# Hybrid state-space and attention layer on one core: state-space products with 512-column high parts, gate sigmoids taken at the merge, two heads' outputs summed together

## The chip, the core and the metric

The program runs on one core of a Trainium2 chip. The core has a matrix engine (TensorE, in profile rows PE, its weight loads PEld), three engines for element-wise work (VectorE = DVE, ScalarE = ACT, GpSimd = POOL) and DMA queues (SP's carries the weights here, POOL's most of the rest). Each engine works through its own list of instructions in order; semaphores tie the lists together. The metric is the device time of one execution in microseconds (us).

## The reference

One decoder layer on 256 tokens of width 2048, all in float32. The part that matters here:

```python
h = rmsnorm(x, attn_norm_w)
z, xbc, dt_raw, q, k, v, g = split(h @ w_in)
xbc = silu(causal_dwconv(xbc, conv_w, conv_b))           # 4 taps along the tokens
xs, Bm, Cm = split(xbc)                                  # 4096 + 1024 + 1024 channels
y = (cb * decay) @ (xs * dt) + xs * d_skip               # per group of 8 heads; head width 64
yg = y * silu(z); yg = yg * rsqrt(mean(yg*yg) + eps) * norm_w
y_ssm = yg @ w_ssm_out
g_ssm, g_attn = split(sigmoid(g + b_gate))
x = x + (g_ssm * y_ssm + g_attn * y_attn) @ w_out
x = x + ffn(rmsnorm(x))                                  # up, 3-tap conv, silu gate, down
```

There are 8 groups of the state-space branch. Each has 4 tiles of z, 4 of xs, one of B and one of C, every tile 128 channels by 256 tokens. `cb * decay` is the 256x256 lower-triangular matrix of a head.

## The kernel before

**Products in three parts.** A float32 weight w is split into a rounded high part (`whi`, made by ACT, L198) and the rest (`wlo`, made by DVE, L199). The activations are split in the same way. A product is high·high + high·low + low·high, each in the fast float32 mode of TensorE. A "unit" (`cm_unit`, L243) is one 128-channel output tile: one weight tile of 128x2048 (1 MB) arrives in `wraw`, is split in two halves ("chunks") of 1024 columns, and each chunk is 8 weight blocks of 128x128. `cm_chunk` (L226) multiplies them in one of two forms:

- *narrow* (`wide=False`): per high block two matmuls of 256 columns, first against the activations' high part (L237), then against their low part (L238), both added into one 256-column result;
- *wide*: per high block one matmul of 512 columns (L234), which holds the high part's product in columns 0 to 255 of a PSUM bank and the low part's in columns 256 to 511. The two halves must be added afterwards by whoever reads the result.

In both forms the 8 low blocks then follow with one matmul of 256 columns each (L240). `wraw`, `whi` and `wlo` have three buffers each, counted in weight tiles for the first and in chunks for the other two; the results (`mm`) have four PSUM banks, and four more (`cc`) serve the state-space core.

**Stages.** Values, queries, keys and attention; the attention gates and the attention output (wide); then the state-space stage, about 455 to 1183 us of the span; then the output projection and the feed-forward network (both wide).

**The state-space stage** is a loop of nine steps (from L944). Step s < 8 computes the ten units of group s (`group_units`, L776), all narrow. The four z units (i < 4) are copied out by ACT (L781). The other six go through the 4-tap convolution: ACT writes the last tap plus bias (L785), and DVE adds three shifted taps (L788). While step s runs, the core of group s-1 is spread over its units, one entry of a list of 14 (`core_steps`, L792) per unit: SiLU of the group's ten tiles, with table loads on ACT (L798, L800); transposes; the decay matrices (`dec`, L842 on: Relu, Exp, multiply by `cb`, split into `mhl`); and `ydot` (L866), which multiplies them with xs for two heads at a time. `ydot(0)` to `ydot(3)` follow units 4, 6, 8 and 9. Per head it reads a PSUM bank with two interleaved halves: 64 partitions hold the head's high and low sums, the other 64 partitions a third part, and DVE adds x·d_skip and the three (L877, L879, L880), on 64 partitions each. Then comes the group's RMS norm. In steps 1, 2 and 8 there are also 4, 4 and 8 units for the state-space gates (`gate_ssm`, L932): ACT adds the bias and takes the sigmoid of the first 8 (L939), which go to DRAM in pairs through the buffer `g`; the last 8 stay in `pre[0]` without sigmoid (L936). From step 3 on there are four `out_unit`s per step (w_ssm_out, narrow, unchanged). At the end `merge` (L968) loads the saved gates back, takes the late ones' sigmoid, multiplies and adds.

**What sets the order.** The program is written unit by unit; a scheduler of the framework then orders each engine's list, keeping the order in which buffers are handed out. The buffer `g` (three of 256 KB) is shared by the attention gates, the state-space gates and the merge.

Of the kernel before, what the change touches and what calls it, by code (L numbers as in the profile page):

```python
# [8 lines left out]
F32 = mybir.dt.float32  # L9
F32R = mybir.dt.float32r  # L10
AF = mybir.ActivationFunctionType
# [4 lines left out]
DM, T, DI, G, NS, H, HD, DFF = 2048, 256, 4096, 8, 128, 16, 128, 5632  # L16
# [160 lines left out]
def _body(tc, nc, d, out):  # L177
# [103 lines left out]
    def sm(name, i=0, n=1, rows=slice(0, 128)):  # L281
        o, _ = _SMALL[name]
        return small[rows, o + i:o + i + n]
# [492 lines left out]
    def group_units(g):  # L776
        pr = pre[g % 2]
        for i in range(10):
            ps = cm_unit(d["wssd"][g, i], hnt, wide=False)
            if i < 4:  # L780
                S.activation(pr[:, i], ps, AF.Copy)  # L781
            else:
                ti = 4 * g + i - 4 if i < 8 else (32 + g if i == 8 else 40 + g)
                acc = pr[:, i]
                S.activation(acc, ps, AF.Identity, scale=sm("conv_w", 4 * ti + 3), bias=sm("conv_b", ti))  # L785
                for k in (2, 1, 0):
                    sh = 3 - k
                    V.scalar_tensor_tensor(acc[:, sh:], ps[:, :T - sh], sm("conv_w", 4 * ti + k), acc[:, sh:],  # L788
                                           op0=MUL, op1=ADD)
            yield i  # L790

    def core_steps(g):  # L792
# [73 lines left out]
        def ydot(p):  # L866
            def f():
                m = st.pop(("m", p))
                for h in range(2):
                    pt = c_tile().rearrange("p (t a) -> p t a", a=2)  # L870
                    ps = pt.rearrange("p t a -> p a t")
                    x0, x1 = [st["x"][:, s, p, 2 * h:2 * h + 2].rearrange("p a c -> p (a c)") for s in range(2)]
                    mt = m[:, :, h].rearrange("p a t -> p t a")
                    PE.matmul(pt, x0, mt[:, 0:256], start=True, stop=False)  # L874
                    PE.matmul(pt[:, 128:], x1, mt[:, 256:384], start=False, stop=True)  # L875
                    rs, ls = slice(h * 64, (h + 1) * 64), slice(64 - h * 64, 128 - h * 64)
                    V.scalar_tensor_tensor(yz[rs, p], pr[rs, 4 + p], sm("ssm_d", 4 * g + p, 1, rs), ps[rs, 0],  # L877
                                           op0=MUL, op1=ADD)
                    V.tensor_tensor(yz[rs, p], ps[rs, 1], yz[rs, p], op=ADD)  # L879
                    V.tensor_tensor(yz[rs, p], ps[ls, 0], yz[rs, p], op=ADD)  # L880
                if p % 2:
                    V.tensor_tensor(yz[:, p - 1:p + 1], yz[:, p - 1:p + 1], pr[:, p - 1:p + 1], op=MUL)
            return f
# [46 lines left out]
        return f  # L930

    def gate_ssm(o):  # L932
        pg = cm_unit(d["wgs"][o], hnt, wide=False)
        if o >= 8:

            S.activation(pre[0][:, o - 8], pg, AF.Identity, bias=sm("b_gate", o))  # L936
            return
        g = gate_half(o)
        S.activation(g, pg, AF.Sigmoid, bias=sm("b_gate", o))  # L939
        if o % 2:  # L940
            nc.gpsimd.dma_start(gs[o // 2], gpair.pop(o // 2))

    dt_steps(dt_unit())
# [24 lines left out]
    def merge(u, ps):  # L968
        os_ = slice(2 * u, 2 * u + 2)
        if u < 4:  # L970
            g = gate_pool.tile([128, 2, T], F32, name="g", bufs=3)
            nc.gpsimd.dma_start(g, gs[u])
            late = pre[0][:, 2 * u:2 * u + 2]
            with tc.issue_after(last_rsq[0].ins):
                S.activation(late, late, AF.Sigmoid)
        else:
            g = pre[0][:, 2 * u - 8:2 * u - 6]
# [135 lines left out]
```

## Time and profile before

| | us |
|---|---|
| median of 3 runs (lowest, highest) | 1967.05 (1965.49, 1968.47) |
| the profiled execution, whole | 1965.37 |
| its span on the core | 1963.6 |
| PE / DVE / ACT busy in the span | 1955.8 / 1567.6 / 1207.6 |
| state-space stage, 455.6 to 1182.7: PE / DVE / ACT busy | 725.4 / 629.3 / 503.8 of 727.1 |

The granted TensorE clock was 1.00 in every stretch. The matmul rows overlap each other, since matmuls are pipelined and the ends are modelled: what a matmul costs is read from the distance between starts, not from its own duration. The same holds in part for DVE and ACT, whose neighbouring rows overlap by some tens of ns.

### The profile page before, as it was taken

Reading aid. Unit: us, or ns where it says so; the run is one execution under the profiler, and the core shown is the slowest. Engines: PE = TensorE matmul, PEld = TensorE weight load, DVE = VectorE, ACT = ScalarE, POOL = GpSimd, SP = SyncE. Lnnn points to the kernel's source line nnn. Section 1 sums busy time; section 2 is a strip of 40 time slices with the busy share of each in tenths; the row PEclk is TensorE's granted clock in tenths of the full one; section 3 lists DMA queues with packets and bytes.
Section 4 is the critical chain, followed back from the end, with each engine's and each line's share of the span. In section 5 each row is a group of like instructions: output and inputs, shape, how many; then the busy total and the mean of one; then the engine's idle time right before and its main releaser. Section 6 shows DMA issues by size and latency. Waiting matters only on the chain.

```text
span 1963.6 us, 35306 instructions
## 1 busy us (share of the span) xinstructions
PE 1955.8 (100%) x14323; PEld 1861.7 (95%) x14323; DVE 1567.6 (80%) x2399; ACT 1207.6 (62%) x1758; POOL 78.6 (4%) x100
## 2 busy tenths in 40 slices
PE   9999999999999999999999999999999999999999
PEld 7999999999999999999999999999999999999998
DVE  7588877767798898888989987788888885788665
ACT  6566656545768768667676655576666654566433
POOL 0012210000000000000000000000000000000000
PEclk9999999999999999999999999999999999999999
DMA  8555555766556556555565585555555555555555
GB/s 298 196 196 183 185 181 198 252 220 211 198 193 216 207 209 209 191 199 196 198 206 195 191 284 203 205 194 202 205 194 206 200 197 209 196 200 208 194 194 170
DMA packets 64331, 402.05 MB, mean 205 GB/s; under 512 B 7655, under 2 KB 10264, under 8 KB 20648
## 3 DMA queue, kind: packets, MB, share of 16 engines
q1 hardware_dynamic: 55384, 376.56, 54.6%
q0 software_dynamic: 5760, 18.97, 3.2%
q10 hardware_dynamic: 3024, 4.27, 0.7%
q8 instruction: 112, 1.84, 0.4%
q14 instruction: 51, 0.42, 0.1%
HBM read 394.44 MB, written 5.33 MB: 204 GB/s over the span
## 4 chain that ended last, share of the span: by engine, by line
PE 97%; DVE 2%; ACT 0%; issue 0%; DMA 0%; DVEq 0%; ACTq 0%
PE mm L234 32%; PE mm L240 30%; PE mm L237 14%; PE mm L238 14%; PE mm L407 1%; PE mm L401 1%; PE mm L402 1%; DVE wlo L199 1%; PE cc L874 1%; PE cc L825 0%; PE cc L875 0%; DVE slotA L788 0%; DMA xw<-x 0%; PE cc L253 0%; PE cc L255 0%
## 5 line engine op out<-in xcount | busy, mean ns | idle before, releaser
L198 ACT ACTIVATE whi<-wraw 128x1024 fp32r<-128x1024 f32 (+1 forms) x712 | 742.6, 1048 | 611.7 <-PE mm L234 313.6
L199 DVE TENSOR_TENSOR wlo<-wraw,whi 128x1024 fp32r<-128x1024 f32 (+1 forms) x712 | 863.8, 1219 | 257.5 <-ACT whi L198 248.8
L237 PE MATMUL mm<-hn,whi 128*128 128x256 f32 x1536 | 353.3, 275 | 1.7 <-ACT whi L198 1.6
L238 PE MATMUL mm<-hn,whi 128*128 128x256 f32 x1536 | 353.0, 275 | 0.0
L234 PE MATMUL mm<-fh,whi 128*128 128x512 f32 x1408 | 333.4, 380 | 0.1
L237 PEld LDWEIGHTS mm<-hn,whi 128*128 128x128 f32 x1536 | 294.9, 192 | 2.7 <-ACT whi L198 2.0
L238 PEld LDWEIGHTS mm<-hn,whi 128*128 128x128 f32 x1536 | 295.0, 192 | 0.1
L234 PEld LDWEIGHTS mm<-fh,whi 128*128 128x128 f32 x1408 | 253.3, 190 | 28.6 <-DVE fh L1016 0.5
L240 PE MATMUL mm<-hn,wlo 128*128 128x256 f32 x1536 | 202.9, 275 | 0.0
L240 PEld LDWEIGHTS mm<-fh,wlo 128*128 128x128 f32 x1408 | 184.6, 191 | 9.4
L240 PEld LDWEIGHTS mm<-hn,wlo 128*128 128x128 f32 x1536 | 186.9, 192 | 0.0
L240 PE MATMUL mm<-fh,wlo 128*128 128x256 f32 x1408 | 185.6, 275 | 0.0
L234 PE MATMUL mm<-a,whi 128*128 128x512 f32 x704 | 167.8, 380 | 0.0
L234 PEld LDWEIGHTS mm<-a,whi 128*128 128x128 f32 x704 | 126.0, 190 | 13.7
L237 PE MATMUL mm<-hp,whi 128*128 128x256 f32 x512 | 118.2, 276 | 0.0
L237 PE MATMUL mm<-yt,whi 128*128 128x256 f32 x512 | 117.7, 275 | 0.0
L238 PE MATMUL mm<-hp,whi 128*128 128x256 f32 x512 | 117.7, 275 | 0.0
L238 PE MATMUL mm<-yt,whi 128*128 128x256 f32 x512 | 117.6, 275 | 0.0
L240 PE MATMUL mm<-hp,wlo 128*128 128x256 f32 x768 | 101.4, 275 | 0.0
L238 PEld LDWEIGHTS mm<-yt,whi 128*128 128x128 f32 x512 | 98.3, 192 | 0.3
L237 PEld LDWEIGHTS mm<-yt,whi 128*128 128x128 f32 x512 | 98.3, 192 | 0.3 <-ACT whi L198 0.2
L240 PEld LDWEIGHTS mm<-a,wlo 128*128 128x128 f32 x704 | 93.5, 191 | 5.1
(306 smaller groups left out, 2825.0 us busy)
## 6 DMA issues: line engine op xcount, KB each, us to landing
wraw<-wup SPq DMA_DIRECT2D x88, 1024.0 KB, 4.8
wraw<-wssd SPq DMA_DIRECT2D x80, 1024.0 KB, 4.9
wraw<-wqk SPq DMA_DIRECT2D x32, 1024.0 KB, 4.8
wraw<-wso SPq DMA_DIRECT2D x32, 1024.0 KB, 5.0
wraw<-wd SPq DMA_DIRECT2D x32, 1024.0 KB, 4.8
wraw<-wga SPq DMA_DIRECT2D x16, 1024.0 KB, 4.8
wraw<-wao SPq DMA_DIRECT2D x16, 1024.0 KB, 4.9
wraw<-wgs SPq DMA_DIRECT2D x16, 1024.0 KB, 4.9
```

What stands on the lines that cost most here:

```text
L198: last_hi[0] = S.activation(hi[:, :n // 2], raw[:, s], AF.Copy)
L199: V.tensor_tensor(lo[:, :n // 2], raw[:, s], hi[:, :n // 2].bitcast(F32), op=SUB)
L234: PE.matmul(ps.rearrange("p (h b a) -> p h b a", h=2, a=2), w, x2[:, :, k0 + k].rearrange("p h (a b) -> p h b a", a=2), start=start, stop= ...
L237: PE.matmul(mixed(ps), w, mix(x2[:, 0, k0 + k]), start=start, stop=False)
L238: PE.matmul(mixed(ps), w, mix(x2[:, 1, k0 + k]), start=False, stop=False)
L240: PE.matmul(mixed(ps[:, :T]), lo[:, k * 128:(k + 1) * 128], mix(x2[:, 0, k0 + k]), start=False, stop=last and k == nk - 1)
L401: PE.matmul(mixed(pst[tt]), hph[:, k0 + k, ts], mix(wh), start=first and k == 0, stop=False)
L402: PE.matmul(mixed(pst[tt]), hpl[:, k0 + k, ts], mix(wh), start=False, stop=False)
L407: PE.matmul(mixed(pst[tt]), hph[:, k0 + k, ts], mix(wl), start=False, stop=last and k == 1)
L874: PE.matmul(pt, x0, mt[:, 0:256], start=True, stop=False)
```

## The change

Three things, all in the state-space stage and the merge:

1. The 80 group units and the 16 gate units become wide. So ACT first copies the second half out (new L782), DVE adds the first half to it (new L783), and where there was one reader of PSUM there now is a sum in SBUF. For the z units that sum lies in its final place. For the convolution units it lies in a `g` buffer, from which ACT (new L786) and DVE (new L789) read; these two were at L785 and L788.
2. `ydot` copies each head's 64 own partitions out with ACT (new L880, 64x512) into one `g` buffer for both heads; DVE then adds x·d_skip and the two sums for both heads at once on 128 partitions (new L881, L882), and the third part per head as before (new L885). Six DVE operations for two heads become four.
3. The first 8 gates are stored without sigmoid; `merge` takes it after loading them back (new L977).

```diff
     def group_units(g):
         pr = pre[g % 2]
         for i in range(10):
-            ps = cm_unit(d["wssd"][g, i], hnt, wide=False)
-            if i < 4:
-                S.activation(pr[:, i], ps, AF.Copy)
-            else:
+            ps = cm_unit(d["wssd"][g, i], hnt)
+            acc = pr[:, i]
+            u = acc if i < 4 else base.tile([128, 2, T], F32, name="g", bufs=3)[:, 0]
+            S.activation(u, ps[:, T:], AF.Copy)
+            V.tensor_tensor(u, ps[:, :T], u, op=ADD)
+            if i >= 4:
                 ti = 4 * g + i - 4 if i < 8 else (32 + g if i == 8 else 40 + g)
-                acc = pr[:, i]
-                S.activation(acc, ps, AF.Identity, scale=sm("conv_w", 4 * ti + 3), bias=sm("conv_b", ti))
+                S.activation(acc, u, AF.Identity, scale=sm("conv_w", 4 * ti + 3), bias=sm("conv_b", ti))
                 for k in (2, 1, 0):
                     sh = 3 - k
-                    V.scalar_tensor_tensor(acc[:, sh:], ps[:, :T - sh], sm("conv_w", 4 * ti + k), acc[:, sh:],
+                    V.scalar_tensor_tensor(acc[:, sh:], u[:, :T - sh], sm("conv_w", 4 * ti + k), acc[:, sh:],
                                            op0=MUL, op1=ADD)
...
         def ydot(p):
             def f():
                 m = st.pop(("m", p))
+                t2 = base.tile([128, T, 2], F32, name="g", bufs=3)
+                pss = []
                 for h in range(2):
                     pt = c_tile().rearrange("p (t a) -> p t a", a=2)
-                    ps = pt.rearrange("p t a -> p a t")
+                    pss.append(pt)
...
                     PE.matmul(pt, x0, mt[:, 0:256], start=True, stop=False)
                     PE.matmul(pt[:, 128:], x1, mt[:, 256:384], start=False, stop=True)
+                    rs = slice(h * 64, (h + 1) * 64)
+                    S.activation(t2[rs], pt[rs], AF.Copy)
+                V.scalar_tensor_tensor(yz[:, p], pr[:, 4 + p], sm("ssm_d", 4 * g + p), t2[:, :, 0], op0=MUL, op1=ADD)
+                V.tensor_tensor(yz[:, p], yz[:, p], t2[:, :, 1], op=ADD)
+                for h in range(2):
                     rs, ls = slice(h * 64, (h + 1) * 64), slice(64 - h * 64, 128 - h * 64)
-                    V.scalar_tensor_tensor(yz[rs, p], pr[rs, 4 + p], sm("ssm_d", 4 * g + p, 1, rs), ps[rs, 0],
-                                           op0=MUL, op1=ADD)
-                    V.tensor_tensor(yz[rs, p], ps[rs, 1], yz[rs, p], op=ADD)
-                    V.tensor_tensor(yz[rs, p], ps[ls, 0], yz[rs, p], op=ADD)
+                    V.tensor_tensor(yz[rs, p], pss[h][ls, :, 0], yz[rs, p], op=ADD)
...
     def gate_ssm(o):
-        pg = cm_unit(d["wgs"][o], hnt, wide=False)
-        if o >= 8:
-
-            S.activation(pre[0][:, o - 8], pg, AF.Identity, bias=sm("b_gate", o))
-            return
-        g = gate_half(o)
-        S.activation(g, pg, AF.Sigmoid, bias=sm("b_gate", o))
-        if o % 2:
+        pg = cm_unit(d["wgs"][o], hnt)
+        g = gate_half(o) if o < 8 else pre[0][:, o - 8]
+        S.activation(g, pg[:, T:], AF.Identity, bias=sm("b_gate", o))
+        V.tensor_tensor(g, pg[:, :T], g, op=ADD)
+        if o < 8 and o % 2:
             nc.gpsimd.dma_start(gs[o // 2], gpair.pop(o // 2))
...
             with tc.issue_after(last_rsq[0].ins):
+                S.activation(g, g, AF.Sigmoid)
                 S.activation(late, late, AF.Sigmoid)
```

Where the instructions then stand, at two places. The first is ACT's list at the end of group 2, from the last convolution unit to the first gate unit. `mm` is a unit's result, `whi` a chunk's high part, `slotA` the group's ten tiles, `sqt1` part of the group norm, `g` in row L939 a gate. Before:

```order
L785 ACTIVATE slotA_5135<-mm_7541,small_63 128x256
L198 ACTIVATE whi_7683<-wraw_7677 128x1024
L798 ACT_TABLE_LOAD
L798 ACTIVATE slotA_5135<-slotA_5135 128x2560
L888 ACTIVATE sqt1_7608<-slotA_5135 128x512
L939 ACT_TABLE_LOAD
L939 ACTIVATE g_7675<-mm_7626,small_63 128x256
L306 ACTIVATE nsp_7613<-sqt0_7607 128x256
L198 ACTIVATE whi_7740<-wraw_7738 128x1024
```

Now (here `g` in L782 and L786 is the convolution's sum, in L880 `ydot`'s copy, in L940 a gate):

```order
L782 ACTIVATE g_7120<-mm_7087 128x256
L880 ACTIVATE g_7127<-cc_7128 64x512
L880 ACTIVATE g_7127<-cc_7132 64x512
L786 ACTIVATE slotA_5135<-g_7120,small_63 128x256
L198 ACTIVATE whi_7202<-wraw_7196 128x1024
L799 ACT_TABLE_LOAD
L799 ACTIVATE slotA_5135<-slotA_5135 128x2560
L893 ACTIVATE sqt1_7142<-slotA_5135 128x512
L940 ACTIVATE g_7193<-mm_7160,small_63 128x256
L198 ACTIVATE whi_7244<-wraw_7242 128x1024
```

One operation per unit and two per `ydot` stand ahead of the next split L198, and L786 must wait for DVE's add between it and L782. The table load in front of the gate is gone. Over the whole program ACT's table loads go from 35 to 23.

The second place is DVE's list for the same unit 9 of group 2 and its `ydot(3)`. Before:

```order
L199 TENSOR_TENSOR wlo_7680<-wraw_7677,whi_7679 128x1024
L788 SCALAR_TENSOR_TENSOR slotA_5135<-mm_7541,small_63,slotA_5135 128x255
L877 SCALAR_TENSOR_TENSOR slotA_5135<-pre1_5136,small_63,cc_7594 64x256
L788 SCALAR_TENSOR_TENSOR slotA_5135<-mm_7541,small_63,slotA_5135 128x254
L879 TENSOR_TENSOR slotA_5135<-cc_7594,slotA_5135 64x256
L788 SCALAR_TENSOR_TENSOR slotA_5135<-mm_7541,small_63,slotA_5135 128x253
L880 TENSOR_TENSOR slotA_5135<-cc_7594,slotA_5135 64x256
L877 SCALAR_TENSOR_TENSOR slotA_5135<-pre1_5136,small_63,cc_7600 64x256
L199 TENSOR_TENSOR wlo_7684<-wraw_7677,whi_7683 128x1024
L879 TENSOR_TENSOR slotA_5135<-cc_7600,slotA_5135 64x256
L880 TENSOR_TENSOR slotA_5135<-cc_7600,slotA_5135 64x256
```

Now:

```order
L199 TENSOR_TENSOR wlo_7199<-wraw_7196,whi_7198 128x1024
L783 TENSOR_TENSOR g_7120<-mm_7087,g_7120 128x256
L881 SCALAR_TENSOR_TENSOR slotA_5135<-pre1_5136,small_63,g_7127 128x256
L882 TENSOR_TENSOR slotA_5135<-slotA_5135,g_7127 128x256
L789 SCALAR_TENSOR_TENSOR slotA_5135<-g_7120,small_63,slotA_5135 128x255
L885 TENSOR_TENSOR slotA_5135<-cc_7128,slotA_5135 64x256
L789 SCALAR_TENSOR_TENSOR slotA_5135<-g_7120,small_63,slotA_5135 128x254
L885 TENSOR_TENSOR slotA_5135<-cc_7132,slotA_5135 64x256
L789 SCALAR_TENSOR_TENSOR slotA_5135<-g_7120,small_63,slotA_5135 128x253
L887 TENSOR_TENSOR slotA_5135<-slotA_5135,pre1_5136 128x512
L199 TENSOR_TENSOR wlo_7203<-wraw_7196,whi_7202 128x1024
```

The three taps L789 now stand behind the add L783 and behind the two 128-partition operations of `ydot`, and the second chunk's split L199 behind all of them. TensorE's list keeps its order of units and core matmuls; each pair of rows L237 and L238 of these units becomes one row L234. On POOL's queue the loads of the saved gates (L972, new L974) stood among the loads of the groups' decay rows (L839, new L840); now they all stand behind the last of those.

## The prediction

> **What bounds the kernel now.** I read the page first: shares per engine, the costliest groups, the chain that ended last.
>
> ```profile
> PE 1955.8 (100%) x14323; PEld 1861.7 (95%) x14323; DVE 1567.6 (80%) x2399; ACT 1207.6 (62%) x1758; POOL 78.6 (4%) x100
> L237 PE MATMUL mm<-hn,whi 128*128 128x256 f32 x1536 | 353.3, 275 | 1.7 <-ACT whi L198 1.6
> PE 97%; DVE 2%; ACT 0%; issue 0%; DMA 0%; DVEq 0%; ACTq 0%
> ```
>
> TensorE is busy for the whole span and makes 97% of the chain. The 1536 rows L237 are the first of the two narrow high products in the 96 units that change (96 units x 16 blocks). A share is an average, so I read the windows of three steps of the state-space stage next (columns: busy time and count of PE, PEld, DVE, ACT, POOL, then clock, DMA share, GB/s), and TensorE's waits in the middle one.
>
> ```profile
> 591.00:672.00 81.00, 79.42 (x702) 78.97 (x702) 68.68 (x101) 62.66 (x86) 4.09 (x8) 1.00 0.59 201
> 832.00:911.50 79.50, 79.50 (x705) 79.25 (x704) 70.36 (x104) 55.11 (x77) 2.16 (x4) 1.00 0.59 200
> PE mm L237 <- ACT whi L198: 1.6, 1, 1.6
> ```
>
> Step 4 (832 to 911.5) has no idle TensorE; step 2 (591 to 672) has one wait of 1.6 us, for a high part that ACT had not split. DVE has 9 us to spare in step 4, ACT 24 us, and DMA a share of 0.59. So here the program costs what TensorE's list costs, plus such waits.
>
> **The matmuls.** A chunk's cost is the distance between equal points of neighbouring chunks: first two narrow chunks of a group unit (the start of the eight low products), then two wide chunks of the feed-forward stage (the start of the eight high products).
>
> ```profile
> 801.45 1.06 PE L240 MATMUL mm<-hn,wlo 128*128 128x256 f32 x8
> 804.13 1.06 PE L240 MATMUL mm<-hn,wlo 128*128 128x256 f32 x8
> ...
> 1401.61 1.89 PE L234 MATMUL mm<-fh,whi 128*128 128x512 f32 x8
> 1403.34 1.05 PE L240 MATMUL mm<-fh,wlo 128*128 128x256 f32 x8
> 1404.23 1.89 PE L234 MATMUL mm<-fh,whi 128*128 128x512 f32 x8
> ```
>
> Narrow: 804.13 - 801.45 = 2.68 us. Wide: 1404.23 - 1401.61 = 2.62 us, of which the high part 1.73 us (216 ns per block) and the low part 0.89. With the same 0.89 the narrow high part is 1.79 us, 224 ns per pair of matmuls. So halving the number of matmuls saves only 0.06 us per chunk, since 512 columns still stream: 96 units x 2 x 0.06 = **11.5 us**. The starts are printed to 0.01 us, so 0.06 may be 0.05 to 0.07: 9.6 to 13.4 us.
>
> The Trainium skill ("TensorE: Matmul & The Clock Gate", Back-to-back issue gap) gives an isolated gap of N/2.4 + 2.5 ns, so two matmuls of 256 columns would lose only 2.5 ns to one of 512; by it the gain would be an estimated 3.8 us. The trace agrees with its value for 512 columns (216 ns) and not with that for 256 (109 against 112).
>
> **What the other engines get.** The prices:
>
> ```profile
> L781 ACT ACTIVATE slotA<-mm 128x256 f32<-128x256 f32 x16 | 5.8, 365 | 0.0
> L785 ACT ACTIVATE slotA<-mm,small 128x256 f32<-128x256 f32 x24 | 13.1, 547 | 0.0
> L1056 ACT ACTIVATE c<-u,small 128x256 f32<-128x256 f32 x88 | 51.4, 584 | 1.8 <-DVE u L1054 1.8
> L927 ACT ACTIVATE slotA<-mm 128x512 f32<-128x512 f32 x8 | 4.7, 581 | 0.0
> L939 ACT ACT_TABLE_LOAD x6 | 7.7, 1283 | 0.1
> L984 ACT ACTIVATE mt<-g 128x512 fp32r<-128x512 f32 x8 | 5.1, 636 | 2.3 <-DVE g L983 2.3
> L1053 DVE TENSOR_TENSOR u<-mm,u 128x256 f32<-128x256 f32 x88 | 36.7, 417 | 0.0
> L788 DVE SCALAR_TENSOR_TENSOR slotA<-mm,small,slotA 128x255 f32<-128x255 f32 (+2 forms) x72 | 34.2, 474 | 0.8
> L877 DVE SCALAR_TENSOR_TENSOR slotA<-pre,small,cc 64x256 f32<-64x256 f32 x32 | 15.2, 475 | 0.5
> L879 DVE TENSOR_TENSOR slotA<-cc,slotA 64x256 f32<-64x256 f32 x64 | 26.7, 417 | 1.1
> L880 DVE TENSOR_TENSOR slotA<-cc,slotA 64x256 f32<-64x256 f32 x64 | 27.0, 422 | 2.0
> L199 DVE TENSOR_TENSOR wlo<-wraw,whi 128x1024 fp32r<-128x1024 f32 (+1 forms) x712 | 863.8, 1219 | 257.5 <-ACT whi L198 248.8
> L862 DVE TENSOR_TENSOR mhl<-m,mhl 128x768 fp32r<-128x768 f32 x32 | 30.3, 956 | 0.5
> L861 ACT ACTIVATE mhl<-m 128x768 fp32r<-128x768 f32 x32 | 27.0, 844 | 9.0 <-DVE m L857 8.5
> L882 DVE TENSOR_TENSOR slotA<-slotA 128x512 f32<-128x512 f32 x8 | 5.5, 687 | 0.1
> ```
>
> DVE: every unit gets an add, 96 x 0.417 = +40.0 us. A `ydot` cost 2 x (0.475 + 0.417 + 0.422) = 2.63 us and now costs 0.475 + 3 x 0.42 = 1.74 us (64 partitions take as long as 128, see L879 and L1053): 32 x -0.89 = -28.5. The taps, read from SBUF, stay near 0.474. Net +11.5 us over the stage.
>
> ACT: 48 copies at 0.365 = +17.5; the bias operation now reads SBUF, bounded by L1056, 48 x 0.037 = +1.8; 64 copies of 64x512, priced by L927 as partitions cost nothing, 64 x 0.581 = +37.2; four sigmoids at the merge, near L984, +2.5; 12 table loads fewer, -15.4. Net +43.6 us.
>
> For a step such as step 4 that is DVE 70.4 + 10 x 0.417 - 4 x 0.89 = 71.0 and ACT 55.1 + 6 x 0.40 + 8 x 0.581 = 62.2, in 79.5 - 1.2 = 78.3 us of TensorE. Both stay below, so on average none of this is on the path. The cover for ACT's and DVE's added work is TensorE's stream itself, which runs behind the splits by the `whi` and `wlo` buffers: a split can start when TensorE has left the high part of the chunk three before (0.89 us before that chunk ends) and is needed two chunks later, 2 x 2.68 + 0.89 = 6.25 us on, of which the split takes 1.05. That leaves **5.2 us of lead** for a late ACT. If it is used up, every further us is TensorE's.
>
> **Where the lead is used up.** At the end of each group ACT waits for the last tap, loads a table, takes SiLU of ten tiles, and splits nothing meanwhile. This is the timeline of step 2, from the last convolution unit to the next split (start, duration, engine, line, operation; in brackets the idle time before and what ended it):
>
> ```profile
> 650.25 0.55 ACT L785 ACTIVATE slotA<-mm,small 128x256 f32<-128x256 f32 x1
> 652.62 1.07 ACT L198 ACTIVATE whi<-wraw 128x1024 fp32r<-128x1024 f32 x1 [1.82 <-PE mm L238]
> 655.56 1.28 ACT L798 ACT_TABLE_LOAD   x1 [1.87 <-DVE slotA L788]
> 656.85 2.35 ACT L798 ACTIVATE slotA<-slotA 128x2560 f32<-128x2560 f32 x1
> 659.38 0.63 ACT L888 ACTIVATE sqt<-slotA 128x512 f32<-128x512 f32 x1 [0.18 <-DVE slotA L882]
> 660.03 1.28 ACT L939 ACT_TABLE_LOAD   x1
> 661.70 0.41 ACT L306 ACTIVATE nsp<-sqt 128x256 fp32r<-128x256 f32 x1
> 662.01 2.94 ACT L198 ACTIVATE whi<-wraw 128x1024 fp32r<-128x1024 f32 x3
> 653.51 0.48 DVE L788 SCALAR_TENSOR_TENSOR slotA<-mm,small,slotA 128x255 f32<-128x255 f32 x1
> 655.02 0.47 DVE L788 SCALAR_TENSOR_TENSOR slotA<-mm,small,slotA 128x253 f32<-128x253 f32 x1
> ```
>
> ACT was done with its part of the unit at 650.80, but DVE, working off arrears, came to the first tap at 653.51. The gap between splits, 652.62 to 662.01, is the one TensorE waited 1.6 us for. After the change two things move it. The gate's table load is gone: 1.28 us earlier, and L306, which overlapped its neighbours to 0.3, stands behind the splits, together -1.6. The last tap comes later: from DVE's arrival at the unit (653.51) to the last tap's end was 655.02 + 0.47 - 653.51 = 1.98 us; now it is the add 0.42, the bias operation 0.58 on ACT (beside which DVE does L881 and L882, 0.9), then three taps and two adds spaced as now, about 1.9: 3.2 us. DVE should arrive about 0.3 us earlier: from unit 4 to 9 it has 6 x 0.417 more and 4 x 0.89 less to do, -1.1 us, while TensorE is 6 x 0.12 = 0.7 faster. So SiLU comes 3.2 - 2.0 - 0.3 = **0.9 us later**. In step 2: 1.6 + 0.9 - 1.6 + 0.1 (two faster chunks) = 1.0 us of wait. In step 3, without gates, nothing is taken back, and the lead was gone already: the split ended at 742.77, and the chunk whose low part starts at 744.72 began its high part 1.79 before, at 742.93.
>
> ```profile
> 741.72 1.05 ACT L198 ACTIVATE whi<-wraw 128x1024 fp32r<-128x1024 f32 x1
> 744.72 1.06 PE L240 MATMUL mm<-yt,wlo 128*128 128x256 f32 x8
> ```
>
> so I charge 1.0 us there, and 0.5 for the steps 4 to 7, whose SiLU came sooner. New waits 2.5, old 1.6: **+0.9 us**. Bounds: no wait at all (-1.6), since DVE's arrears may go; and 2.6 us of delay per group end, that of two more full turns between ACT and DVE with 1.3 us each, so about 2.7 in steps 2 and 3 and 0.5 in four others, +5.8.
>
> The gates' DMAs: the writes stay four, and the loads now stand behind the last decay row on POOL's queue, but the first is needed only after the 12 units of step 8, 12 x 5.3 = 64 us; nothing waits. The `g` buffer gives each tile to its third successor, about two units (10 us) later, more than its readers need; if not, ACT's copy waits for the tap of an older unit, and the lead pays.
>
> **Sum.** Profiled execution 1965.37 - 11.5 + 0.9 = 1954.8; the median of the runs shown is 1.7 above that execution, so **1956.5 us** (-0.54%).
>
> **Rivals.** *A, arrears on DVE:* units 4 to 9 ask DVE for 12 x 1.22 + 6 x 0.417 + 18 x 0.474 + 4 x 1.74 + 2 x 0.956 + 2 x 0.687 = 36 us, against 6 x 5.24 + 4 x 2 x (0.216 + 0.111) = 34 of TensorE, and in the turn ACT-DVE-ACT-DVE it may idle 0.65 us per unit, 3.9 per step. For: the arrears of 2.7 us shown above, before any idling. Against: in four of six units L881 and L882 fill the turn. Price: about 1.3 us of wait in six steps, 8 us: 1965.37 - 11.5 + 8 + 1.7 = 1963.6, almost no change.
>
> *B, ACT's list blocks, slower:* ACT now stands in front of its splits until DVE has done L783. ACT's work in units 4 to 9 is 12 x 1.06 + 6 x 0.95 + 8 x 0.58 + 2 x 0.844 + 0.63 = 25.3 us; with a wait W per unit it is 25.3 + 6W against 34 of TensorE and about 4 of lead, so W = 2.1 us decides. With arrears of 2.7 us and the add of 0.42, W = 3.1 and 6 us are lost per step, in seven steps 41: about 1997; at W = 2.5 it is 16 us and 1972. Against: in the feed-forward stage the same hand-over stays short and TensorE never waits:
>
> ```profile
> 1404.86 0.36 ACT L1052 ACTIVATE u<-mm 128x256 f32<-128x256 f32 x1
> 1405.83 0.42 DVE L1053 TENSOR_TENSOR u<-mm,u 128x256 f32<-128x256 f32 x1
> ```
>
> that is W = 1405.83 + 0.42 - 1405.22 = 1.0 us, and arrears of 2.7 us come only at a group's end.
>
> *C, the pairs were not dearer:* if the 0.06 us were not the form but the operand (`hn` against `fh`), the gain falls to nothing and the waits stay: 1968. The wide form reads the same columns there and here. The skill's gap formula of the same page would put the time at an estimated 1964 to 1965; the two chunk distances above speak against it.
>
> **How the numbers follow.** Forecast 0.75, A 0.13, B 0.08, C 0.04. The likeliest time is the sum, 1956.5; its own range is 1953 (no waits left, 1967.05 - 11.5 - 1.6 = 1954, and 0.07 per chunk) to 1962 (upper bound of the waits). The range for 8 in 10 adds most of A: 1953 to 1964.5. About 0.2%, 3.9 us, can be told from no change here: faster means under 1963.1. Faster: the forecast's 0.75 plus a third of A, about 0.80; same: the rest of A and C, 0.13; slower 0.07.
>
> **What would show it.** In the profile of the changed kernel: rows L234 with `hn` 1536 times, chunk to chunk 2.62 us; the state-space stage near 716 us; PE still 100% and waits of PE for `whi` of about 2 to 3 us in total, at the group ends of steps 2 and 3; DVE about 1579 and ACT about 1251 us busy; no table load at the gates. Wrong it is if waits of PE for `whi` or `wlo` sum to over 6 us (A, B), above all behind ACT's L786, or if the distance stays 2.68 (C).

## The result, and the profile after

| | before | after |
|---|---|---|
| median of 6 runs (lowest, highest), us | 1966.61 (1965.3, 1968.47) | 1955.57 (1954.76, 1956.24) |
| the profiled execution, whole | 1965.37 | 1956.12 |
| its span | 1963.6 | 1954.3 |
| ratio of the medians, 95% interval | | 0.9944 (0.9931 to 0.9957) |

The changed kernel is faster by 0.56%, 11.0 us in the medians. The two profiled executions lie 9.25 us apart: that of before lay 1.24 us below its median, that of after 0.55 us above its own. Here are the page's lines on the engines, on the new high product and on the chain that ended last.

```profile
PE 1945.7 (100%) x12787; PEld 1808.8 (93%) x12787; DVE 1570.2 (80%) x2431; ACT 1242.8 (64%) x1862; POOL 78.5 (4%) x100
L234 PE MATMUL mm<-hn,whi 128*128 128x512 f32 x1536 | 363.6, 380 | 1.1 <-ACT whi L198 1.1
PE 96%; DVE 2%; issue 1%; ACT 1%; DMA 0%; POOL 0%; ACTq 0%; DVEq 0%; POOLq 0%
```

TensorE has 1536 matmuls fewer and is 10.1 us less busy; it is still 100% busy and 96% of the chain. DVE got only 2.6 us more work, ACT 35.2.

TensorE's timeline at the end of group 1, around the first wait that it now has, gives the new distance of two chunks (start, duration, line; in brackets an idle time and what ended it):

```profile
573.64 1.05 PE L240 MATMUL mm<-hn,wlo 128*128 128x256 f32 x8
...
576.26 1.05 PE L240 MATMUL mm<-hn,wlo 128*128 128x256 f32 x8
...
581.02 1.99 PE L234 MATMUL mm<-hn,whi 128*128 128x512 f32 x8 [1.09 <-ACT whi L198]
```

576.26 - 573.64 = 2.62 us, where the narrow form had 2.68. One chunk on comes a wait of 1.09 us for a high part. All waits of TensorE from the start of the state-space stage to the end of the merge (us in total, times, longest):

```profile
PE mm L234 <- ACT whi L198: 1.1, 1, 1.1
PE mm L237 <- ACT whi L198: 0.7, 1, 0.7
PE mm L234 <- DVE mt L988: 0.6, 1, 0.6
PE cc L254 <- DVE bcl L805: 0.3, 1, 0.3
```

They sum to 2.7 us; before there was one, of 1.6. Read from TensorE's timeline, the first stands at the end of step 1 (581.02), the last at the end of step 0 (524.06). The other two, at 1156.83 and 1180.61, stand in the merge and at the start of the output projection. None is left at the ends of steps 2 to 7.

The stage, from its first dt row (L739) to the first matmul of the output projection (operand `mt`), took 727.8 us before (455.6 to 1183.4) and 717.2 now (455.8 to 1173.0): 10.6 less. From there to the first matmul of the feed-forward stage (operand `fh`) it took 83.9 and now 85.0: 1.1 more. So almost the whole gain lies in the stage, and some is given back behind it.

The window of step 4 (columns as in the prediction):

```profile
829.00:907.30 78.30, 78.30 (x545) 73.75 (x544) 70.44 (x105) 61.48 (x90) 2.15 (x4) 1.00 0.57 204
```

DVE does 70.44 us of work in 78.30 of TensorE and ACT 61.48; the prediction had 71.0 and 62.2.

**The group end.** This is ACT's timeline at the end of groups 1 and 2: the copy of the last unit's result (L782) and the table load ahead of SiLU (L799).

```profile
569.08 0.38 ACT L782 ACTIVATE g<-mm 128x256 f32<-128x256 f32 x1
...
575.37 1.28 ACT L799 ACT_TABLE_LOAD   x1 [1.73 <-DVE pre L789]
...
648.23 0.38 ACT L782 ACTIVATE g<-mm 128x256 f32<-128x256 f32 x1
...
653.25 1.28 ACT L799 ACT_TABLE_LOAD   x1 [1.63 <-DVE slotA L789]
```

From the copy to the table load it is 575.37 - 569.08 = 6.29 us in step 1 and 653.25 - 648.23 = 5.02 in step 2. Worked out in the same way for every step (before, the bias operation L785 stands where the copy stands now; the last row belongs to the first experiment):

| copy of unit 9 to SiLU's table load, us | step 0 | 1 | 2 | 3 | 4 | 5 | 6 | 7 |
|---|---|---|---|---|---|---|---|---|
| before | 2.86 | 3.80 | 5.31 | 5.31 | 3.64 | 3.64 | 3.65 | 3.65 |
| after | 5.36 | 6.29 | 5.02 | 4.98 | 4.99 | 5.02 | 4.98 | 4.98 |
| after, with the old `ydot` | 5.36 | 6.44 | 7.50 | 7.52 | 7.50 | 7.53 | 7.57 | 7.59 |

Before, steps 2 and 3 carried arrears of DVE. After, no step from 2 on carries any: the chain of add, bias operation and taps takes its own 5.0 us there. Step 1 takes 1.3 us more; why DVE is later there no run shows.

**The merge.** ACT's timeline there:

```profile
1138.99 1.08 ACT L198 ACTIVATE whi<-wraw 128x1024 fp32r<-128x1024 f32 x1 [0.69 <-PE mm L238]
1146.24 0.63 ACT L977 ACTIVATE g<-g 128x512 f32<-128x512 f32 x1 [6.17 <-DMA g<-gs]
1146.78 1.04 ACT L198 ACTIVATE whi<-wraw 128x1024 fp32r<-128x1024 f32 x1
...
1154.68 0.63 ACT L977 ACTIVATE g<-g 128x512 f32<-128x512 f32 x1 [4.45 <-DMA g<-gs]
...
1155.74 1.99 ACT L198 ACTIVATE whi<-wraw 128x1024 fp32r<-128x1024 f32 x2
```

The new sigmoid L977 stands in ACT's list ahead of splits, and its operand is a gate that is still on its way from DRAM. For 6.17 us, and then for 4.45, ACT does nothing, and the splits behind it come late. POOL's timeline shows when the loads were issued, and for what they had waited:

```profile
1139.66 0.54 POOL L974 DMA_DIRECT2D g<-gs  x1 [1.69 <-DVE mt L988]
...
1149.97 0.54 POOL L974 DMA_DIRECT2D g<-gs  x1 [6.88 <-DVE mt L988]
```

They wait for a free `g` buffer, which DVE gives back when the merge of an earlier pair is done. Before the change these loads were about as late (1151.31 and 1156.67), but then only a multiply of DVE's needed them, and no split stood behind it; DVE's waits there name no load.

### The profile page after: what moved, and what is told of

Same layout as the page of the kernel before. It is cut to its first block, busy times and chain, and to the rows that moved or that the text cites. A ratio compares the mean times of both kernels' runs of the same rounds, so it can differ in the third digit from the quotient of the medians.

```text
span 1954.3 us, 32426 instructions
## 1 busy us (share of the span) xinstructions
PE 1945.7 (100%) x12787; PEld 1808.8 (93%) x12787; DVE 1570.2 (80%) x2431; ACT 1242.8 (64%) x1862; POOL 78.5 (4%) x100
## 4 chain that ended last, share of the span: by engine, by line
PE 96%; DVE 2%; issue 1%; ACT 1%; DMA 0%; POOL 0%; ACTq 0%; DVEq 0%; POOLq 0%
PE mm L234 48%; PE mm L240 30%; PE mm L237 6%; PE mm L238 5%; PE mm L407 1%; PE mm L401 1%; PE mm L402 1%; DVE wlo L199 1%; PE cc L877 1%; PE cc L878 0%; PE cc L826 0%; ACT whi L198 0%; DMA g<-gs 0%; DVE pre L789 0%; PE cc L254 0%
## 5 line engine op out<-in xcount | busy, mean ns | idle before, releaser
L198 ACT ACTIVATE whi<-wraw 128x1024 fp32r<-128x1024 f32 (+1 forms) x712 | 741.7, 1046 | 520.4 <-PE mm L234 338.3
L199 DVE TENSOR_TENSOR wlo<-wraw,whi 128x1024 fp32r<-128x1024 f32 (+1 forms) x712 | 863.1, 1219 | 243.7 <-ACT whi L198 236.2
L234 PE MATMUL mm<-hn,whi 128*128 128x512 f32 x1536 | 363.6, 380 | 1.1 <-ACT whi L198 1.1
L234 PE MATMUL mm<-fh,whi 128*128 128x512 f32 x1408 | 333.3, 379 | 0.1
L234 PEld LDWEIGHTS mm<-hn,whi 128*128 128x128 f32 x1536 | 276.1, 190 | 32.9 <-ACT whi L198 1.3
L234 PEld LDWEIGHTS mm<-fh,whi 128*128 128x128 f32 x1408 | 253.1, 190 | 28.8 <-DVE fh L1019 0.5
L240 PEld LDWEIGHTS mm<-hn,wlo 128*128 128x128 f32 x1536 | 201.3, 191 | 10.3
L234 PE MATMUL mm<-a,whi 128*128 128x512 f32 x704 | 167.9, 379 | 0.0
L234 PEld LDWEIGHTS mm<-a,whi 128*128 128x128 f32 x704 | 125.9, 190 | 13.7
L237 PE MATMUL mm<-yt,whi 128*128 128x256 f32 x512 | 117.8, 275 | 0.7 <-ACT whi L198 0.7
L237 PE MATMUL mm<-hp,whi 128*128 128x256 f32 x512 | 118.2, 276 | 0.0
L238 PE MATMUL mm<-hp,whi 128*128 128x256 f32 x512 | 117.6, 275 | 0.0
L238 PE MATMUL mm<-yt,whi 128*128 128x256 f32 x512 | 117.6, 275 | 0.0
L237 PEld LDWEIGHTS mm<-yt,whi 128*128 128x128 f32 x512 | 98.3, 192 | 1.2 <-ACT whi L198 1.1
L238 PEld LDWEIGHTS mm<-yt,whi 128*128 128x128 f32 x512 | 98.3, 192 | 0.3
L237 PEld LDWEIGHTS mm<-hp,whi 128*128 128x128 f32 x512 | 98.3, 192 | 0.1
L238 PEld LDWEIGHTS mm<-hp,whi 128*128 128x128 f32 x512 | 98.3, 192 | 0.1
```

Source lines behind the costliest of these rows:

```text
L198: last_hi[0] = S.activation(hi[:, :n // 2], raw[:, s], AF.Copy)
L199: V.tensor_tensor(lo[:, :n // 2], raw[:, s], hi[:, :n // 2].bitcast(F32), op=SUB)
L234: PE.matmul(ps.rearrange("p (h b a) -> p h b a", h=2, a=2), w, x2[:, :, k0 + k].rearrange("p h (a b) -> p h b a", a=2), start=start, stop= ...
L237: PE.matmul(mixed(ps), w, mix(x2[:, 0, k0 + k]), start=start, stop=False)
L238: PE.matmul(mixed(ps), w, mix(x2[:, 1, k0 + k]), start=False, stop=False)
L240: PE.matmul(mixed(ps[:, :T]), lo[:, k * 128:(k + 1) * 128], mix(x2[:, 0, k0 + k]), start=False, stop=last and k == nk - 1)
```

## Experiments

All times are medians in us. "Before" is the kernel before, run on the same chip beside the experiments: 1965.62 for the first four, 1966.21 for the next four, 1965.59 for the last. The kernel after has 1955.57; it was not run again beside them, and the kernel before differs by up to 1 us from round to round. So a difference to after of 2 us rests on the traces as well as on the medians.

| kernel | median | ratio to before (95%) |
|---|---|---|
| after, with the old `ydot` | 1976.11 | 1.0052 (1.0039 to 1.0064) |
| after, with the gates' sigmoid in its old place | 1962.98 | 0.9985 (0.9976 to 0.9994) |
| before, with only the new `ydot` | 1963.80 | 0.9989 (0.9980 to 0.9997) |
| before, with only the 32 z units wide | 1962.71 | 0.9985 (0.9976 to 0.9994) |
| after, gates loaded into other buffers at the merge | 1953.51 | 0.9934 (0.9921 to 0.9948) |
| after, SiLU of eight tiles one unit earlier | 1962.07 | 0.9979 (0.9970 to 0.9988) |
| after, one more pass of ACT ahead of SiLU | 1966.21 | 0.9999 (0.9990 to 1.0008) |
| the fifth and the sixth together | 1959.72 | 0.9966 (0.9953 to 0.9978) |
| the fifth, and query and key units wide | 1966.22 | 1.0004 (0.9995 to 1.0013) |

### The 32 z units alone: what a chunk is worth

The prediction's main term is 0.06 us per chunk. The z units are where the wide form costs least elsewhere: no taps follow.

```diff
-            ps = cm_unit(d["wssd"][g, i], hnt, wide=False)
+            ps = cm_unit(d["wssd"][g, i], hnt, wide=i < 4)
             if i < 4:
-                S.activation(pr[:, i], ps, AF.Copy)
+                S.activation(pr[:, i], ps[:, T:], AF.Copy)
+                V.tensor_tensor(pr[:, i], ps[:, :T], pr[:, i], op=ADD)
```

> The kernel before with only the 32 z units wide (32 of the 96), which have no convolution behind them. Theory: 32 units x 2 chunks x 0.06 us = -3.8 us, as DVE has room in units 0 to 3 of a step: 1962.8 us. Rival with a pair of matmuls only 2.5 ns dearer than one of 512 columns: -1.3 us, 1965.3. Rival with the gain coming from somewhere else (waits, DVE): no change, 1966.6.

Measured: 2.9 us less than before. TensorE's waits in this kernel's stage:

```profile
PE mm L237 <- ACT whi L198: 1.7, 2, 1.5
PE mm L240 <- DVE wlo L199: 0.6, 2, 0.3
```

That is 2.3 us against 1.6 before. So the 64 chunks gave 2.9 + 0.7 = 3.6 us, 0.056 each (by the interval of the ratio, 0.03 to 0.085). The Trainium skill's formula ("TensorE: Matmul & The Clock Gate", Back-to-back issue gap) would give an estimated 1.3 us for them, 0.020 each; this run does not agree with it. The rival that narrow pairs are not dearer falls too.

### The old `ydot` back: are the arrears real?

```diff
-                    rs = slice(h * 64, (h + 1) * 64)
-                    S.activation(t2[rs], pt[rs], AF.Copy)
-                V.scalar_tensor_tensor(yz[:, p], pr[:, 4 + p], ..., t2[:, :, 0], op0=MUL, op1=ADD)
-                V.tensor_tensor(yz[:, p], yz[:, p], t2[:, :, 1], op=ADD)
...
+                    V.scalar_tensor_tensor(yz[rs, p], pr[rs, 4 + p], ..., ps[rs, 0], op0=MUL, op1=ADD)
+                    V.tensor_tensor(yz[rs, p], ps[rs, 1], yz[rs, p], op=ADD)
+                    V.tensor_tensor(yz[rs, p], ps[ls, 0], yz[rs, p], op=ADD)
```

> The changed kernel with the old ydot (three DVE operations per head on 64 partitions, no copies by ACT). Theory (TensorE sets the pace, DVE's arrears at a group's end decide how late SiLU and the next split come): DVE gets 8 groups x 3.6 = 28.5 us back on, units 4 to 9 of a step ask it for 39.6 us against 34 of TensorE, SiLU comes up to 3.5 us later, and with leads of 0 to 0.9 us left at the group ends of steps 1 to 7 that is 2 to 3.3 us of wait in each: 1968 us (1962 to 1977). Rival (DVE's average decides: about 74.6 us of work in 78.3 us of TensorE per step): no change, 1955.5 us.

Measured: 1976.11, 20.5 us more than after and 10.5 more than before. The same 11.5 us of matmul time are saved, and more than that is lost. TensorE's waits in this kernel's stage and merge:

```profile
PE mm L237 <- ACT whi L198: 9.6, 6, 1.9
PE mm L240 <- DVE wlo L199: 2.6, 2, 1.9
PE mm L234 <- ACT whi L198: 2.0, 1, 2.0
...
```

With two short ones they sum to 15.1 us against 2.7, and one stands at the end of each of the seven groups from step 1 on. ACT's timeline at the end of group 3 shows why:

```profile
728.77 0.36 ACT L782 ACTIVATE g<-mm 128x256 f32<-128x256 f32 x1
733.15 0.60 ACT L786 ACTIVATE pre<-g,small 128x256 f32<-128x256 f32 x1 [4.01 <-DVE g L783]
...
736.29 1.28 ACT L799 ACT_TABLE_LOAD   x1 [1.59 <-DVE pre L789]
```

After its copy ACT stands for 4.01 us in front of L786, because DVE comes that late to the add. SiLU then starts 7.52 us after the copy instead of 4.98, and about as late at the ends of steps 2 to 7 (last row of the table above): 2.5 us of arrears. Over a step DVE would have had room: four old `ydot`s cost 4 x 0.89 = 3.6 us more, on 70.4 of 78.3. So the average does not decide. What decides is the stretch from unit 4 to unit 9, where the convolution and `ydot` fall together. The rivals of DVE's arrears and of ACT's blocked list are one mechanism, it is real, and the new `ydot` holds it off. The size was underestimated: the theory said 1968, and part of the rest (5 us) is the granted clock, shown in the last section.

### The new `ydot` alone

> The kernel before with the new ydot alone, everything narrow. Theory: no matmul is saved and DVE's relief of 28.5 us is off TensorE's path; only the waits at group ends can move, by -1.6 to +1 us: 1965 to 1967.6 us, no change. Rival (DVE's relief is where the change gains): 1960 us or less.

The edit is the second part of the change, put into the kernel before, with all units narrow. Measured: 1963.80, 1.8 us less than before. TensorE has no wait at all in this kernel's stage; the 1.6 us at the end of step 2 are gone. That is a little more than the theory allowed (1965 at the least), and far from its rival. It is all that the relief of DVE is worth when nothing else is added: the same edit is worth 20.5 us when the wide units are there.

### The sigmoid back at the gate

```diff
         V.tensor_tensor(g, pg[:, :T], g, op=ADD)
+        if o < 8:
+            S.activation(g, g, AF.Sigmoid)
...
-                S.activation(g, g, AF.Sigmoid)
```

> The changed kernel with the first eight gates' sigmoid taken in the gate unit again (after the add, in place), none of it at the merge. Theory: the merge no longer blocks ACT behind the load of a gate, -1.8 us; but the gate's table load and the sigmoid stand in front of the next split at the group ends of steps 1 and 2, which have no lead, +1.7 us each: 1957 us. Rival (table loads lie beside other work): only the merge's part is seen, 1953.8 us.

Measured: 1962.98, 7.4 us more than after; the theory had 1.4, and its rival a gain. The waits of TensorE in the stage and merge of this kernel:

```profile
PE mm L234 <- ACT whi L198: 3.5, 6, 1.2
PE mm L240 <- DVE wlo L199: 3.4, 2, 1.7
PE mm L237 <- ACT whi L198: 1.1, 1, 1.1
...
```

With a short one 8.3 us, none of them in the merge, where after has 1.1 and 0.3 outside the merge. ACT's timeline in the middle of step 1 of it:

```profile
598.65 1.28 ACT L943 ACT_TABLE_LOAD   x1
...
602.30 1.28 ACT L857 ACT_TABLE_LOAD   x1
```

The sigmoid needs another table than the group core around it, so a load goes there and one back, close behind each other, and in steps 1 and 2 that happens inside a unit as well as at the group end. Two waits of 1.7 us (at 613.49 and 696.01) are for low parts: DVE, made late by ACT, is late with `wlo`. So the third part of the change is worth 7.4 us: about 9.5 at the gates, less the 2.1 that the sigmoid's new place costs, as the next run shows. The run brings back the twelve table loads and the eight sigmoids together; what each costs alone was not tried.

### The gates loaded into other buffers

```diff
-            g = gate_pool.tile([128, 2, T], F32, name="g", bufs=3)
+            g = sd.tile([128, 2, T], F32, name="ab", bufs=2)
```

In `merge` only: the saved gates go into the two buffers of the decay rows, which are free by then.

> The changed kernel with the saved gates loaded into the two buffers of the decay rows (free by then) instead of the three shared ones, so that the merge's new sigmoid finds them loaded. Theory: in the changed kernel ACT sat 6.2 and 4.5 us behind the loads of two gates, and TensorE then waited 0.66 us (high part), 0.61 us (merge result) and lost some 0.5 us more in rows without a named wait; all of it goes: -1.7 us, 1953.9. Rival (the waits come from ACT's and DVE's work at the merge, not from the load): no change, 1955.6.

Measured: 1953.51 (1953.09 to 1953.94), 2.1 us less than after, all its runs below all those of after. This is the fastest version. TensorE's waits in its stage and merge:

```profile
PE mm L234 <- ACT whi L198: 1.0, 1, 1.0
PE cc L254 <- DVE bcl L805: 0.3, 1, 0.3
```

Both of the merge are gone. ACT's timeline at the two sigmoids whose gates came late in after:

```profile
1140.55 0.64 ACT L977 ACTIVATE ab<-ab 128x512 f32<-128x512 f32 x1 [0.31 <-DMA ab<-gs]
...
1146.23 0.64 ACT L977 ACTIVATE ab<-ab 128x512 f32<-128x512 f32 x1 [0.63 <-DMA ab<-gs]
```

ACT waits 0.31 and 0.63 us instead of 6.17 and 4.45. That settles the merge: the load's wait for a `g` buffer, passed on through ACT's list, cost TensorE 2.1 us. (The edit also leaves all three `g` buffers to the merge's other loads; the two effects were not parted.)

### One more pass ahead of SiLU

```diff
         def silu():
+            S.activation(pr, pr, AF.Copy)
             last = S.activation(pr, pr, AF.Silu)
```

The pass changes no value and takes ACT 2.35 us more at each of the eight group ends.

> The changed kernel with one more pass of ACT over the group's ten tiles (a copy onto itself, 2.35 us) ahead of each SiLU: the block at each group end is made longer by a known amount. Theory: the leads of high parts left there in the changed kernel are 0 (end of step 1), 0.1, 0.2, 0.2, 0.9, 0.9, 0.9 us for steps 1 to 7 and 2.1 for step 0; what is over becomes TensorE's wait: 2.35 x 7 - 3.2 + 0.2 = 13.4 us, 1969 us. Rival (TensorE has more in store than the leads say, or ACT's average decides): below 1960 us.

Measured: 1966.21, 10.6 us more than after, the whole gain of the change. TensorE's waits:

```profile
PE mm L237 <- ACT whi L198: 7.0, 6, 2.0
PE mm L234 <- ACT whi L198: 1.1, 3, 0.5
...
```

With two short ones 9.1 us against 2.7, and 1.7 more were lost to the granted clock (last section). But the block at the group end did not simply get longer. This is ACT's timeline at the end of group 5 (the pass, a split, SiLU, the next splits):

```profile
893.29 2.36 ACT L799 ACTIVATE pre<-pre 128x2560 f32<-128x2560 f32 x1 [1.63 <-DVE pre L789]
...
896.08 1.04 ACT L198 ACTIVATE whi<-wraw 128x1024 fp32r<-128x1024 f32 x1
...
898.43 2.34 ACT L800 ACTIVATE pre<-pre 128x2560 f32<-128x2560 f32 x1
...
900.98 2.00 ACT L198 ACTIVATE whi<-wraw 128x1024 fp32r<-128x1024 f32 x2
```

The scheduler put a split between the pass and SiLU; at the ends of groups 1 to 4 there are two. So the block was cut in two and not lengthened by 2.35 us, and the theory's 13.4 us were not put to the test. At the ends of groups 5 to 7 TensorE waited 1.8 to 2.0 us for the split behind SiLU (902.07, 982.51, 1063.08); at groups 1 to 4 each wait is under 0.5 us, even at group 1, where after has 1.1. What the run does show is that 8 x 2.35 = 18.8 us more work of ACT, which is idle for 712 us of after's span, cost 10.6 us.

### SiLU in two pieces

```diff
+            if i == 8:
+                S.activation(pr[:, 0:8], pr[:, 0:8], AF.Silu)
...
-            last = S.activation(pr, pr, AF.Silu)
+            last = S.activation(pr[:, 8:10], pr[:, 8:10], AF.Silu)
```

> The changed kernel with SiLU of a group's first eight tiles (and its table load) taken after unit 8, so that only two tiles' SiLU stand between the last tap and the next split. Theory (the group end's block on ACT, about 4.5 us, is what eats the lead): the block shrinks by some 3 us, the 1.09 us wait at the end of step 1 goes, and no other comes: 1954.4 us. Rival (ACT's work in units 4 to 9, 25 of 34 us, has no room for 3.2 us more at unit 8): the waits move to units 8 and 9, 1956 to 1960 us.

Measured: 1962.07, 6.5 us more than after. The rival was right in kind, though its range ended at 1960. The waits moved from the high parts to the low ones:

```profile
PE mm L240 <- DVE wlo L199: 6.6, 8, 1.3
...
```

Two of these eight stand at the end of group 1 (573.63 and 577.80), and one at the end of each of groups 2 to 7. DVE's timeline near the end of group 1 of this kernel has the reason:

```profile
567.71 0.42 DVE L783 TENSOR_TENSOR g<-mm,g 128x256 f32<-128x256 f32 x1 [2.46 <-ACT g L782]
```

While ACT loads the table and takes SiLU (564.20 to 567.41 on its timeline), the next unit's copy stands behind it. DVE idles for 2.46 us at the place where it has no time to lose, and its splits come late. With the better gate buffers the loss is the same:

> The gate buffers and the split SiLU together, on the changed kernel. Theory: both gains add, -1.7 and -1.2 us: 1952.7 us, TensorE without a wait in the state-space stage. Rival: as in the two single runs where one of them fails.

Measured: 1959.72, 6.2 us more than with the buffers alone. So ACT's time at the group end is not simply too long in one piece; a piece moved ahead stalls DVE.

### The query and key units wide

With the fifth experiment's kernel as the base, the 32 narrow units of queries and keys were made wide.

```diff
-            evac(key, i % 2, cm_unit(d["wqk"][j, i], hp2, wide=False))
+            evac(key, i % 2, cm_unit(d["wqk"][j, i], hp2))
...
+            n = st["n" + key][:, h]
+            S.activation(halves(n), unmix(ps[:, T:]), AF.Copy)
+            V.tensor_tensor(halves(n), unmix(ps[:, :T]), halves(n), op=ADD)
+            S.activation(st["s" + key][:, h], n, AF.Square)
+            S.activation(n, n, AF.Copy, scale=sm("qn") if key == "q" else kscale)
```

> The gate-buffer kernel with the 32 query and key units wide too (one copy by ACT and one add by DVE more per unit, square and scale then read SBUF). Theory, from the same matmul price: 32 x 2 x 0.06 = -3.8 us against the gate-buffer kernel (1953.5 us), so 1949.7, if DVE, with 86 of 100 us busy there before and 13.3 us more to do in about 170, still keeps its lead: then it has 93 to 94. Rival (as with the old ydot: what counts is DVE's arrears in a burst, not its average): waits of TensorE for low parts eat it, 1953 to 1960 us.

Measured: 1966.22, 12.7 us more than its base, where 3.8 less were hoped for. The longest entry of TensorE's waits over the whole program:

```profile
PE cc L499 <- DVE part L494: 11.9, 5, 2.5
```

Neither expectation had this place. L499 is a small matmul for the queries' and keys' norm. It has its fixed place in TensorE's list, and the chain to it (copy, add, square, partial sum) got two links longer. No split is late here; the stream itself stops five times at one instruction. Two of these stops (145.83 and 200.61) were followed by half the granted clock, which cost about 3.4 us more (last section).

## Why the prediction was right, and where it was not

**The pace and the 0.06 us: right.** 1536 rows L234 stand at 2.62 us per chunk, and the z units alone confirm 0.056 us per chunk by a time. The 192 chunks give the 11.5 us of the sum.

**"Net +11.5 us" for DVE and "Net +43.6 us" for ACT: above the page, without effect on the time.** The page has +2.6 and +35.2. That is how the page counts, since neighbouring rows overlap: the durations of the same rows, added up one by one, give +16.9 and +42.7. The operations priced from rows came out near: L880 at 0.586 us against 0.581, L783 at 0.418 against 0.417; DVE's sum is higher since two operations of `ydot` were slower than priced (last section). That both lie below TensorE was right, but "Both stay below, so on average none of this is on the path" decides nothing by itself. With the old `ydot` both also stay below, and 20.5 us are lost.

**"SiLU comes 0.9 us later": wrong in both directions.** Step by step, against before, it came 2.5 us later in steps 0 and 1, 0.3 earlier in steps 2 and 3, and 1.3 to 1.4 later in steps 4 to 7. The working carried DVE's arrears of step 2 on and took off only 0.3 us. The new `ydot` took all of them off, which the third row of the table shows from the other side. So the waits forecast for steps 2 and 3 did not come. In steps 4 to 7 the later SiLU cost nothing where 0.5 in all was charged, since some lead was left. These are, after the change, a split behind SiLU of step 5 and the chunk that it is for:

```profile
891.75 1.04 ACT L198 ACTIVATE whi<-wraw 128x1024 fp32r<-128x1024 f32 x1
...
893.60 0.28 PE L237 MATMUL mm<-yt,whi 128*128 128x256 f32 x1
```

The split ended at 892.79 and TensorE came at 893.60: 0.8 us of lead. Read in the same way it was 0.1 at step 2, 0.2 at steps 3 and 4, and 0.8 at steps 5 to 7. These leads price a delay: the 2.5 us by which the old `ydot` makes SiLU later, less the leads, are 1.7 to 2.4 us per group end from step 2 on, and the waits there were 1.5 to 2.0. At the end of step 1, where the prediction charged nothing, SiLU came 2.5 us later and TensorE waited 1.1. No lead was left there before the change either: that split began at 580.68 and takes 1.05, and TensorE came at 581.78. The 2.5 us, less the 1.6 that the prediction took off for the missing table load and L306, are 0.9, near the wait that came.

**"The gates' DMAs … nothing waits": the step that failed.** It looked at when the load is needed, 64 us later, and not at what frees its buffer or who stands behind its reader. The sigmoid moved to the merge put the wait for that load into ACT's list, ahead of splits. Charged at 0, it cost 2.1 us by the run with other buffers.

**The sum.** New waits were put at 2.5 us and old ones at 1.6, +0.9. The view of waits has 2.7, and that the two lie so close is luck: none of the waits forecast for steps 2 to 7 came, and none of those that came had been forecast. Around each wait 0.1 to 0.2 us more are lost: summed over the excess of each chunk distance above its normal value, it is about 4.5 us after and 2.4 before: +2.1. So 1965.37 - 11.5 + 2.1 = 1956.0, and measured was 1956.12 where the prediction had 1954.8 for this execution. The median fits better than the sum did, 1955.57 against 1956.5. The 1.7 us added for the median were right for before (1.24 with all six runs) and did not apply to after, whose profiled execution lay 0.55 us above its median. So part of the close fit is misses against each other.

**The table loads: under-priced.** The prediction credited the missing table load, with L306, with 1.6 us in step 2 alone. Putting the sigmoid back, with its loads, cost 7.4 us in time, though ACT got only 17.0 us more work by it (1259.8 against 1242.8).

**Rivals.** Arrears on DVE and the blocked list of ACT did not come: W, the time ACT stands in front of L786, was 35.2 us over 35 times in the stage, 1.0 on average and at most 2.1, the value from which the prediction said it would decide. With the old `ydot` it reached 4.1 and the loss came. The chances of 0.13 and 0.08 were no waste: the margin was one rewritten helper. What no run tried is a longer lead itself, with a fourth buffer of `whi` and `wlo`.

## What to carry to other kernels

When TensorE is 100% busy, a saving on it is real, but it is kept only as far as the engines that feed it stay ahead in the worst few microseconds; price an edit against the lead at that place, with the arrears carried into it, and not against the average over a stage. The same 11.5 us of matmul time gave a gain of 11.0 us, 2.6 us or a loss of 10.5, depending on how `ydot` was written and where eight sigmoids stood; alone, the new `ydot` was worth 1.8. And before an operation that reads a load is given to an engine, look at what stands behind it in that engine's list, and at what frees the load's buffer.

## What the runs showed of the hardware

**The granted clock fell after waits of under 2 us.** With the old `ydot`, TensorE waited 1.94 us at the end of group 3 and then did this (its timeline):

```profile
741.93 0.38 PE L237 MATMUL mm<-yt,whi 128*128 128x256 f32 x1 [1.94 <-ACT whi L198]
...
743.03 0.28 PE L238 MATMUL mm<-yt,whi 128*128 128x256 f32 x1
743.14 0.37 PE L237 MATMUL mm<-yt,whi 128*128 128x256 f32 x1
743.31 0.42 PE L238 MATMUL mm<-yt,whi 128*128 128x256 f32 x1
...
746.67 0.27 PE L238 MATMUL mm<-yt,whi 128*128 128x256 f32 x1
746.78 0.28 PE L237 MATMUL mm<-yt,whi 128*128 128x256 f32 x1
```

For 1.1 us after the wait the matmuls follow each other at 0.11 us. From 743.2 to 746.6, about 3.4 us, they follow at 0.21, half the rate, and then at 0.11 again: 1.7 us lost. The windows of the same kernel have it as the granted clock (the column behind POOL's):

```profile
743.20:746.60 3.40, 3.40 (x18) 3.40 (x18) 2.54 (x3) 3.37 (x4) 0.00 (x0) 0.50 0.30 53
825.12:828.52 3.40, 3.40 (x18) 3.40 (x17) 2.71 (x4) 3.37 (x5) 0.00 (x0) 0.50 0.23 43
1067.46:1070.87 3.41, 3.41 (x18) 3.41 (x17) 3.19 (x5) 3.38 (x5) 0.00 (x0) 0.50 0.42 91
```

Just before and just behind each of these three stretches the clock is 1.00.

It happened after three of the seven group ends of that kernel (741.93, 824.01 and 1066.36), about 5 us in all, and not after the others, whose waits were as long (1.5 to 2.0 us). It happened once with the extra pass (after the wait at 1063.08) and twice with the wide query units; in the kernels before and after the clock is 1.00 throughout. So a wait near 2 us can cost almost twice its length, and whether it does is not told by its length.

Its place tells more. The three stretches are 3.41 us long, and their starts lie 81.92 and 242.34 us apart, 24 and 71 times 3.413 us: they lie on one grid of time. Counted on that grid, the waits before them (1.94, 1.92 and 1.82 us) each lay whole inside one period of 3.413 us, and the half rate began with the next period. Of the other four waits, those that end at 661.68 and 986.01 (2.03 and 1.81 us) lay across a border, with at most 1.63 in one period; the other two had 1.74 and 1.47 in one. With the wide query units, stops of 2.53 and 2.25 us inside one period were followed by half rate, and 2.24, 2.31 and 2.52 across a border were not. One wait does not fit: with the extra pass, 1.86 of the 1.89 us that end at 982.51 lay in one period, and the clock stayed. How much of a period must be idle, these runs leave open.

The Trainium skill ("TensorE: Matmul & The Clock Gate", What's actually happening) tells of a clock gate that goes to half rate by the activity in a free-running window of 3413 ns. The half rate, the 3.4 us and a window that runs freely agree with these rows. Its limit for idle gaps, about 3.4 us, does not agree: waits of 1.8 to 1.9 us were enough here. No run moved a wait on the grid to test it.

**Reading every second element seems to cost a little.** In the new `ydot`, the two operations that read every second element of the copy in SBUF took 0.52 (L881) and 0.46 us (L882), against the 0.475 and 0.42 that the prediction had taken from operations that read PSUM. The taps L789, which read SBUF without a stride, take 0.478. The stride alone was not tried.
